# VectorE's order written out around the last depthwise tiles and the first layer norm of a Conformer block

## The chip, the cores and the metric

The kernel runs on one core of one Trainium2 chip. The metric is device time in microseconds of one execution. Three runs of the kernel before gave 2790.43, 2791.1 and 2793.83 us; their median is 2791.1 us.

## The reference

One inference step of a two-layer backbone for 1024 sample tokens and 128 prompt tokens, 1024 features, all in float32. Layer 0 mixes tokens with a Conformer convolution, layer 1 with attention; each is followed by a convolutional feed-forward. The change lies in the Conformer convolution:

```
def conformer_conv(h, w_pw1, dw_w, dw_b, ln_g, ln_b, w_pw2):
    a, g = jnp.split(h @ w_pw1, 2, axis=-1)
    u = a * jax.nn.sigmoid(g)
    u = dwconv(u, dw_w, dw_b)                       # 31 taps over the tokens, feature by feature
    u = jax.nn.silu(layernorm(u, ln_g, ln_b))       # mean and variance over the 1024 features
    return u @ w_pw2
```

A token's layer norm needs all 1024 features, so it can begin only when the depthwise convolution of all features has reached that token. After this, the result goes through `x = x + g1 * y`, a norm, and the feed-forward.

## The kernel before, in words

**Layout.** Features lie on the 128 partitions in 8 tiles (`KT`), tokens along the columns in 3 chunks of 384 (`CH`, `NCH`); chunk 2 ends with the prompt. Matrix products are made to float32 precision from three products of a high and a low part (`mm3`, lines 247 to 249: hi x hi, hi x lo, lo x hi), so every operand of a product exists as a pair `hh`, `hl`. A product of one weight (128 output features) with one chunk is 24 matmuls.

**Depthwise stage.** For tiles 0 to 6, 12 taps run on ScalarE and GpSimd (`taps_pool`, lines 645 to 651) into `pacc`, and 19 on VectorE (`taps_vector`, lines 658 and 660) into `da`, an accumulator of three PSUM banks (tag `acc`, one buffer). `join` (line 666) adds the two and writes `U[c][:, j, :]` for each chunk. For tile 7, the last, 16 taps are matmuls with diagonal matrices (line 706) into one PSUM bank per chunk, `dl[c]` (tag `mm`, four banks, which pw2's products and the layer norm use too), 8 taps run on ScalarE and GpSimd, and 7 on VectorE on top of `dl[c]`, chunk by chunk.

**Layer norm.** The sums for the mean are matmuls with a constant matrix (line 722), seven for the first seven tiles of each chunk, written in the program before any layer norm step. Chunk 0 has its own bank for them; chunks 1 and 2 share a tile of the tag `acc`, which is free when tile 6 has been joined. `layer_norm(c)` then adds the last tile's term (line 726), subtracts the mean in two halves (line 731), squares on ScalarE (line 738, tag `tmp`, two buffers, shared with the squares of pw2's statistics), adds the squares on VectorE for one half and on GpSimd for the other (lines 741 and 744), sums them over the partitions with small matmuls (line 325), raises to the power -0.5 on GpSimd (line 334), spreads the result over the partitions (line 342), scales (line 753), applies Silu (line 757), makes the high part (line 760) and the low part (line 762). It is a generator: `tick()` advances every such generator in `bg` by one step, up to its next `yield`. While the taps of tile 7 for chunk c+1 are written, the norm of chunk c is advanced by one step after each tap.

**After it.** `project_residual` makes the pw2 products (named pw2p in the profile) chunk by chunk and adds them to x (line 384). x comes back from DRAM chunk by chunk (`reload`, line 388) into the place of `U[c]`, so it waits until the layer norm of chunk c is done with it.

**What sets the order.** Every engine works through its own list in order. The lists are made at compile time by a planner that plays the program through with estimated costs and puts an instruction in when its inputs are ready. SyncE's list (all loads of weights and of x) is in the order of the program throughout (`manual_schedule`), TensorE's in the attention alone; within such a region the named engines keep the program's order, and the others stay with the planner. VectorE's list is the planner's everywhere. Next weights are loaded three ahead and split into high and low parts one ahead (lines 209, 220, 221).

Of the kernel before, what the change touches and what calls it, by code (L numbers as in the profile page):

```python
# [16 lines left out]
P = 128  # L17
# [5 lines left out]
CH = 384  # L23
# [40 lines left out]
def raw32(t):  # L64
    return t.bitcast(F32)


def pieces(c):
    """A chunk's columns by the conditioning of their tokens."""
    lo, hi = c * CH, (c + 1) * CH  # L70
    out = []
    if lo < NS:
        out.append((0, min(hi, NS) - lo, 0))
    if hi > NS:
        out.append((max(lo, NS) - lo, CH, 1))
    return out
# [3 lines left out]
def tile_hybrid_step(ctx: ExitStack, tc: tile.TileContext, a: dict, outs: list):  # L80
# [17 lines left out]
    def phase(**slots):  # L98
        """SBUF of a phase: so many tiles of so many columns for each tag."""
        stack = ExitStack()  # L100
        pools = {
            tag: (stack.enter_context(tc.tile_pool(name=f"s_{tag}", bufs=bufs, reuse_waits="tile")), n)
            for tag, (bufs, n) in slots.items()
        }

        def tile_(tag, name, dt=F32, n=None):
            pool_, cols_ = pools[tag]
            return pool_.tile([P, n or cols_], dt, tag=tag, name=name)

        return stack, tile_  # L110
# [15 lines left out]
    class Banks:  # L126
        """PSUM, cut anew for some phases."""

# [16 lines left out]

    # work that runs beside the products, a step after each of them
    bg = []
# [22 lines left out]

    # ---- weights, in the order of their use: loads run up to three tiles ahead, the split into hi + lo (both exact
    # in float32r) one or two ----
    def ffn_order(l):
# [25 lines left out]
    class Weights:  # L199
# [24 lines left out]
        def ahead(self, splits, loads):  # L224
            """Has everything up to so many tiles from the next one split or loaded."""
            for i in range(self.at, min(self.at + max(splits, loads), len(self.order))):
                if self.order[i][0] == "stop":
                    break
                if i < self.at + loads and i not in self.raw and i not in self.ready:
                    self.load(i)  # L230
                if i < self.at + splits and i not in self.ready:
                    self.split(i)
# [17 lines left out]

# [1 line left out]
    def ada(pool, l, grp):  # L252
# [55 lines left out]

# [1 line left out]
    def add_stat(acc, j, c, src, eng=None, tag=None):  # L310
# [8 lines left out]
    def token_rstd(pool, parts, name, bank=None):  # L319
        """Sums over features of all parts[f, token], then (mean + eps) ** -0.5, tokens on partitions."""  # L320
        n = CH // P
        ps = pool("ms", f"{name}_s") if bank is None else bank[:, CH:]
        for t in range(n):
            for i, x in enumerate(parts):
                nc.tensor.matmul(
                    ps[:, t : t + 1], x[:, t * P : (t + 1) * P], ones, start=(i == 0), stop=(i == len(parts) - 1)
                )
        return rstd_of(ps[:, 0:n], 1.0 / D, n, name)
# [8 lines left out]
    def spread(pool, v, name, bank=None):  # L337
        """v[token, t] to every partition, tokens along the columns."""
        n = v.shape[1]
        ps = pool("ms", f"{name}_b") if bank is None else bank  # L340
        for t in range(n):
            nc.tensor.matmul(
                ps[:, t * P : (t + 1) * P], v[:, t : t + 1].to_broadcast([P, P]), ident, start=True, stop=True
            )
        return ps[:, 0 : n * P]
# [44 lines left out]

# [1 line left out]
    def ffn(pool, H, X, l, name, beside, done):  # L392
# [87 lines left out]

    # =========================== layer 0 ===========================
    pool.open(mm=(4, 512), acc=(1, 1536), ms=(1, 512))

# [1 line left out]
    vec_rows = [  # L485
# [36 lines left out]
    def load_x(c):  # L522
        """A chunk's tokens, on partitions, where the low parts of the normed chunks go later."""
        n = CH // P
        toks = hp.tile([P, n, D], F32, tag="hl", name=f"xt{c}")
        for t in range(n):
            tt = c * n + t
            nc.sync.dma_start(
                toks[:, t, :], a["x_sample"][0, tt * P : (tt + 1) * P, :] if tt < NS // P else a["x_prompt"][0]
            )  # L530
        return toks
# [45 lines left out]

    # conformer: gated pointwise, depthwise over tokens, layernorm, silu, pointwise
    us = []

    def gated(j, c):
        """The products of a chunk; yields before their gating."""
        if c == 0:
# [58 lines left out]
    def taps_pool(j, u, pacc, t0, s0_, s1_):  # L642
        """The taps from t0 on, with the bias."""
        d = pacc[:, s0_:s1_]
# [8 lines left out]
    def taps_vector(j, u, d, n, s0_, s1_, fresh):  # L653
        """The first n taps."""
        for t in range(n):
            src = u[:, s0_ + t : s1_ + t]
            if t == 0 and fresh:
                nc.vector.tensor_scalar(d, src, tap(j, t), None, ALU.mult)
            else:
                nc.vector.scalar_tensor_tensor(d, src, tap(j, t), d, ALU.mult, ALU.add)  # L660
            yield
# [9 lines left out]
    for j in range(last + 1):  # L671
# [14 lines left out]
        taps_pool(j, u, pacc, t0, 0, CONV_N)  # L686
        for _ in taps_vector(j, u, da[:, 0:CONV_N], t0, 0, CONV_N, True):
            pass
        for c in range(NCH):
            join(j, da, pacc, c)  # L690

    # the last tile: some taps as products with diagonals, the others on top of them, chunk by chunk, so that the norm
    # of a chunk runs beside the taps of the next
    u = us[last][2]
# [6 lines left out]
    for c in range(NCH):  # L701
        s0_, s1_ = SPAN[c]
        dl.append(pool("mm", f"dl{c}")[:, 0 : s1_ - s0_])
        for i in range(PE_TAPS):
            t = te + i
            nc.tensor.matmul(
                dl[c], diag[:, i, :], u[:, s0_ + t : s1_ + t], start=(i == 0), stop=(i == PE_TAPS - 1)
            )

    L = [None] * NCH  # L710
# [13 lines left out]
    def layer_norm(c):  # L724
# [4 lines left out]
        for g in range(2):  # L729
# [3 lines left out]
            )  # L733
            eng = (nc.vector, nc.gpsimd)[g]
            for i in range(half // 2):
                sq = slot("tmp", f"lnsq{c}_{g}_{i}")[:, 0 : 2 * CH]
# [8 lines left out]
            yield  # L745
        yield
        bank = pool("mm", f"lnv{c}")
        rs = token_rstd(pool, ss, f"lnv{c}", bank)
        yield
        pb = spread(pool, rs, f"lnv{c}", bank)  # L750
        for g in range(2):
            jj = slice(g * half, (g + 1) * half)
            nc.vector.tensor_tensor(
                U[c][:, jj, :], U[c][:, jj, :], pb.unsqueeze(1).to_broadcast([P, half, CH]), ALU.mult
            )
            for j in range(g * half, (g + 1) * half):
                nc.scalar.activation(
                    U[c][:, j, :], U[c][:, j, :], AF.Silu, scale=col("conv_ln_g", j), bias=col("conv_ln_b", j)
                )
            nc.scalar.activation(hh[:, jj, :], U[c][:, jj, :], AF.Copy)  # L760
            yield
            nc.vector.tensor_tensor(hl[:, jj, :], U[c][:, jj, :], raw32(hh)[:, jj, :], ALU.subtract)
# [5 lines left out]
    for c in range(NCH):  # L768
# [4 lines left out]
        if c == 0:  # L773
            tick()

    def project_residual(H, X, c, acc, l, name, tag):
# [29 lines left out]

    # =========================== layer 1 ===========================
    # rotary tables with the norm gains folded in, tokens on partitions; gains: plain, halves swapped and signed
    NB = NS // P + 1
# [59 lines left out]
    def head_norm(ps, which, tt, name):  # L869
        """RMS norm of two heads, rotary unless they are the prompt's; yields between its stages."""  # L870
        ss = tiny(f"{name}ss", 2)
# [37 lines left out]
    def place(b, tt, o):  # L909
        """Heads to [feature, token]."""  # L910
        pt = pool("t", f"ptqk{b}_{tt}")
# [14 lines left out]

    # each slot: the products of a tile, then a further stage of each tile before it, the oldest first
    stages = []
# [50 lines left out]

    # the prompt's queries see the prompt's own keys: the four heads of a group at once  # L980
    def prompt():
# [54 lines left out]

    # samples: blocks of one head and the queries of one chunk, in steps of 128 queries; the scores run two steps
    # ahead of the transposes, the product with V one block behind them
    blocks = [(c, h) for c in range(NCH) for h in range(NH)]
# [27 lines left out]
    def softmax(s, st):  # L1067
        """Yields before each part of its exponential."""
        v = st["v"]
# [121 lines left out]

    # final norm, back to tokens on partitions
    gfs = []
# [44 lines left out]
def _rope_table():  # L1238
    """cos and sin by position on the 64-wide grid: [128, 2, 9, 32]; block t < 8 is the row part of token tile t,
    block 8 the column part, which all tiles share."""  # L1240
    import numpy as np
# [34 lines left out]
```

## Time and profile before

| | us |
|---|---|
| median of three runs | 2791.1 |
| lowest and highest | 2790.43, 2793.83 |
| span of the profiled execution | 2789.3 |
| TensorE busy in the span | 2724.6 (98%) |
| VectorE, ScalarE, GpSimd busy | 1585.4, 1053.5, 699.6 |

The span runs from the first instruction to the last of one profiled execution; a time outside the profile is that of the whole program. Times in the trace are counted from the start of the span. In a timeline row the first number is the start, the second how long the instruction or the merged run of `xN` instructions took, then engine, line, operation and tiles (output<-inputs); brackets give the idle time of the engine before it and who ended it. PE is TensorE (float32 matmuls with plain float32 operands appear as two records each), DVE is VectorE, ACT ScalarE, POOL GpSimd, SPq the queue of SyncE. A busy TensorE need not be at its full clock: the granted clock stands beside it, 1.00 for 2.4 GHz and 0.50 for 1.2 GHz.

### The profile page before, as it was taken

The numbers are of one execution on the slowest core, as the hardware profiler recorded it, in microseconds if no ns is written. First come the engines' busy times: TensorE is split into PE (matmuls) and PEld (weight loads), VectorE is DVE, ScalarE is ACT, GpSimd is POOL, SyncE is SP. The second block draws the span as 40 slices with busy tenths as digits, with TensorE's granted clock in tenths as the row PEclk, the third lists the DMA queues.
The fourth block names the chain that finished last, engine by engine and source line by source line (L and its number), as shares of the span: only waits on it lengthen the run. The fifth ranks groups of instructions, "written<-read, shape, count | busy, mean of one in ns | idle before, by whom it ended". The sixth has DMA issues, their size and how long they took to land.

```text
span 2789.3 us, 40007 instructions
## 1 busy us (share of the span) xinstructions
PE 2724.6 (98%) x15959; PEld 2577.1 (92%) x15959; DVE 1585.4 (57%) x2743; ACT 1053.5 (38%) x2066; POOL 699.6 (25%) x782
## 2 busy tenths in 40 slices
PE   7999989999999999999999899999999999999999
PEld 4867649999999999999999799899999999999998
DVE  6878886544444444445643788766544444444445
ACT  5545546422222221222555777755422122221222
POOL 2777744300000000000555566535000000000003
PEclk9999989999999999999999999999999999999999
DMA  7465425311111111111210000044111111111111
GB/s 261 158 185 160 154 91 176 110 32 46 46 46 46 39 46 38 46 38 46 95 58 1 1 1 1 32 129 136 45 40 46 38 46 39 46 39 45 32 53 69
DMA packets 194419, 192.18 MB, mean 69 GB/s; under 512 B 7072, under 2 KB 173323, under 8 KB 192698
## 3 DMA queue, kind: packets, MB, share of 16 engines
q1 hardware_dynamic: 193946, 189.53, 21.7%
q8 instruction: 126, 2.06, 0.3%
q14 instruction: 59, 0.48, 0.1%
q0 software_dynamic: 288, 0.11, 0.0%
HBM read 175.19 MB, written 14.42 MB: 68 GB/s over the span
## 4 chain that ended last, share of the span: by engine, by line
PE 94%; DVE 3%; DMA 1%; ACT 1%; issue 0%; POOL 0%; SPq 0%; DVEq 0%; ACTq 0%; POOLq 0%
PE f1pd L249 3%; PE f1pd L247 3%; PE f1pd L248 3%; PE f1pg L249 3%; PE f0pg L249 3%; PE f1pg L248 3%; PE f0pg L248 3%; PE f0pv L247 3%; PE f0pg L247 3%; PE f1pv L249 3%; PE f1pg L247 3%; PE f0pv L248 3%; PE f1pv L248 3%; PE f1pv L247 3%; PE f0pv L249 3%; PE f0pd L248 3%
## 5 line engine op out<-in xcount | busy, mean ns | idle before, releaser
L220 ACT ACTIVATE w_hi<-w_raw 128x1024 fp32r<-128x1024 f32 x208 | 218.1, 1058 | 939.4 <-PE f0pd L248 223.7
L221 DVE TENSOR_TENSOR w_lo<-w_raw,w_hi 128x1024 fp32r<-128x1024 f32 x208 | 269.4, 1304 | 425.0 <-ACT w_hi L220 422.4
L651 POOL TENSOR_TENSOR pacc<-pacc,tmp 128x1167 f32<-128x1167 f32 (+2 forms) x98 | 234.2, 2393 | 64.8 <-ACT tmp L650 41.6
L384 DVE SCALAR_TENSOR_TENSOR x<-f1pd,mods,x 128x256 f32<-128x256 f32 (+1 forms) x352 | 170.2, 514 | 102.6 <-PE f1pd L249 102.4
L384 DVE SCALAR_TENSOR_TENSOR x<-f0pd,mods,x 128x256 f32<-128x256 f32 (+1 forms) x352 | 169.8, 514 | 99.1 <-PE f0pd L249 98.9
L660 DVE SCALAR_TENSOR_TENSOR da<-u,dww,da 128x1167 f32<-128x1167 f32 x126 | 180.8, 1435 | 2.8
L1084 POOL TENSOR_TENSOR pr<-pr,sm 128x384 f32<-128x384 f32 x192 | 153.8, 829 | 107.3 <-DVE sm L1082 49.4
L411 POOL MEMSET f1gp<- 128x1 f32 x66 | 3.7, 98 | 703.7 <-DVE f1gp L435 690.5
L411 POOL MEMSET f0gp<- 128x1 f32 x66 | 3.6, 98 | 703.8 <-DVE f0gp L435 690.7
L248 PE MATMUL f1pd<-f1al,w_hi 128*128 128x384 f32 x528 | 178.8, 339 | 0.0
L249 PE MATMUL f1pd<-f1ah,w_lo 128*128 128x384 f32 x528 | 178.7, 338 | 0.0
L249 PE MATMUL f0pd<-f0ah,w_lo 128*128 128x384 f32 x528 | 178.7, 338 | 0.0
L248 PE MATMUL f0pd<-f0al,w_hi 128*128 128x384 f32 x528 | 178.5, 338 | 0.0
L247 PE MATMUL f1pd<-f1ah,w_hi 128*128 128x384 f32 x528 | 178.5, 339 | 0.0
L247 PE MATMUL f0pd<-f0ah,w_hi 128*128 128x384 f32 x528 | 178.0, 338 | 0.0
L249 PE MATMUL f0pg<-n_h,w_lo 128*128 128x384 f32 x528 | 176.7, 335 | 0.0
L249 PE MATMUL f1pg<-n_h,w_lo 128*128 128x384 f32 x528 | 176.7, 335 | 0.0
L248 PE MATMUL f1pg<-n_l,w_hi 128*128 128x384 f32 x528 | 176.7, 335 | 0.0
L248 PE MATMUL f0pv<-n_l,w_hi 128*128 128x384 f32 x528 | 176.7, 335 | 0.0
L248 PE MATMUL f0pg<-n_l,w_hi 128*128 128x384 f32 x528 | 176.7, 335 | 0.0
L247 PE MATMUL f0pg<-n_h,w_hi 128*128 128x384 f32 x528 | 176.7, 335 | 0.0
L247 PE MATMUL f1pg<-n_h,w_hi 128*128 128x384 f32 x528 | 176.7, 335 | 0.0
(327 smaller groups left out, 7802.7 us busy)
## 6 DMA issues: line engine op xcount, KB each, us to landing
adaw<-in_ada_w_dram SPq DMA_DIRECT2D x96, 512.0 KB, 4.4
w_raw<-in_ffn_w_up_dram SPq DMA_DIRECT2D x88, 512.0 KB, 3.8
w_raw<-in_ffn_w_down_dram SPq DMA_DIRECT2D x44, 512.0 KB, 3.9
w_raw<-in_conv_w_pw_dram SPq DMA_DIRECT2D x40, 512.0 KB, 6.8
w_raw<-in_attn_w_o_dram SPq DMA_DIRECT2D x24, 512.0 KB, 4.4
xs_d<-x SPq DMA_DIRECT2D x6, 1536.0 KB, 11.1
x<-xs_d SPq DMA_DIRECT2D x6, 1536.0 KB, 7.8
w_raw<-in_attn_w_qkv_dram SPq DMA_DIRECT2D x12, 512.0 KB, 3.6
```

The lines of the kernel that those rows point to most:

```text
L220: nc.scalar.activation(hi, raw, AF.Copy)
L221: nc.vector.tensor_tensor(lo, raw, raw32(hi), ALU.subtract)
L247: nc.tensor.matmul(ps, wh, mh, start=first, stop=False)
L248: nc.tensor.matmul(ps, wh, ml, start=False, stop=False)
L249: nc.tensor.matmul(ps, wl, mh, start=False, stop=last)
L384: nc.vector.scalar_tensor_tensor(xx, ps[:, lo:hi], mod(l, v, j, cond), xx, ALU.mult, ALU.add)
L411: nc.gpsimd.memset(gp[:, z : z + 1], 0.0)
L651: nc.gpsimd.tensor_tensor(d, d, tmp, ALU.add)
L660: nc.vector.scalar_tensor_tensor(d, src, tap(j, t), d, ALU.mult, ALU.add)
L1084: nc.gpsimd.tensor_tensor(pr[n], pr[n], ri.to_broadcast([P, CH]), ALU.mult)
```

## The change

Three edits; comments and docstrings are taken out besides.

1. From the taps of tile 6 on, up to the end of tile 7's joins, VectorE's list is the order of the program. The VectorE part of tile 6 (19 taps and the joins) is moved in the program behind the products of tile 7 and the diagonal matmuls, to the head of this region. So VectorE makes tile 6 to its end, then the taps of tile 7 for chunk 0 and their join, then the first step of chunk 0's layer norm (line 726, the subtractions), and then the taps of chunk 1, after each of them a step of chunk 0's layer norm, then chunk 2's taps with the steps of chunk 1's.
2. The squares alternate between the two halves, and the subtractions get a step of their own.
3. For chunk 0, scaling, Silu, high and low part go in four parts of two tiles in place of two of four, each low part written after the next part's scaling.

```diff
-        for _ in taps_vector(j, u, da[:, 0:CONV_N], t0, 0, CONV_N, True):
-            pass
-        for c in range(NCH):
-            join(j, da, pacc, c)
+        def on_vector(j=j, u=u, da=da, pacc=pacc, t0=t0):
+            for _ in taps_vector(j, u, da[:, 0:CONV_N], t0, 0, CONV_N, True):
+                pass
+            for c in range(NCH):
+                join(j, da, pacc, c)
+
+        if j < last - 1:
+            on_vector()
...
+    vector = ExitStack()
+    vector.enter_context(tc.manual_schedule(engines={mybir.EngineType.DVE}))
+    on_vector()
+
     L = [None] * NCH
...
-            eng = (nc.vector, nc.gpsimd)[g]
-            for i in range(half // 2):
+        yield
+        for i in range(half // 2):
+            for g in range(2):
+                eng = (nc.vector, nc.gpsimd)[g]
...
             yield
-        yield
         bank = pool("mm", f"lnv{c}")
         rs = token_rstd(pool, ss, f"lnv{c}", bank)
         yield
         pb = spread(pool, rs, f"lnv{c}", bank)
-        for g in range(2):
-            jj = slice(g * half, (g + 1) * half)
+        n = 2 if c == 0 else half
+        for j0 in range(0, KT, n):
+            jj = slice(j0, j0 + n)
             nc.vector.tensor_tensor(
-                U[c][:, jj, :], U[c][:, jj, :], pb.unsqueeze(1).to_broadcast([P, half, CH]), ALU.mult
+                U[c][:, jj, :], U[c][:, jj, :], pb.unsqueeze(1).to_broadcast([P, n, CH]), ALU.mult
             )
...
             nc.scalar.activation(hh[:, jj, :], U[c][:, jj, :], AF.Copy)
-            yield
+            if c or j0 % half:
+                yield
+            if c == 0 and j0:
+                pp = slice(j0 - n, j0)
+                nc.vector.tensor_tensor(hl[:, pp, :], U[c][:, pp, :], raw32(hh)[:, pp, :], ALU.subtract)
+            if c:
+                nc.vector.tensor_tensor(hl[:, jj, :], U[c][:, jj, :], raw32(hh)[:, jj, :], ALU.subtract)
+        if c == 0:
             nc.vector.tensor_tensor(hl[:, jj, :], U[c][:, jj, :], raw32(hh)[:, jj, :], ALU.subtract)
         L[c] = (hh, hl)
...
         if c == 0:
             tick()
+    vector.close()
```

## Rows read from the trace of the kernel before

**Rows 1.** The page's chain of waits, shares of the span by engine.
```profile
PE 94%; DVE 3%; DMA 1%; ACT 1%; issue 0%; POOL 0%; SPq 0%; DVEq 0%; ACTq 0%; POOLq 0%
```

**Rows 2.** Table by stretch: busy us of PE, PEld, DVE, ACT, POOL; clock, DMA.
```profile
402.00:417.00 15.00, 6.18 (x23) 4.92 (x22) 13.06 (x13) 12.81 (x17) 4.02 (x4) 0.50 0.01 2
417.00:422.40 5.40, 5.38 (x17) 5.38 (x18) 2.20 (x2) 5.40 (x8) 0.00 (x0) 0.50 0.51 171
...
422.40:523.70 101.30, 101.30 (x600) 101.30 (x599) 70.93 (x86) 55.98 (x83) 44.22 (x34) 1.00 0.56 169
```

**Rows 3.** Timeline of TensorE, 384 to 417 us.
```profile
384.67 0.81 PE L726 MATMUL mu<-u,mean_w 128*128 128x384 f32 x2
385.32 5.32 PE L722 MATMUL mu<-u,mean_w 128*128 128x384 f32 x16
...
395.53 0.81 PE L726 MATMUL mu<-u,mean_w 128*128 128x384 f32 x2
...
405.87 2.29 PE L325 MATMUL lnv<-ones,lnss 128*128 128x1 f32 x10 [0.28 <-POOL lnss L744]
410.19 1.65 PE L342 MATMUL lnv<-ident,lnv_r 128*128 128x128 f32 x6 [2.02 <-POOL lnv_r L334]
...
417.02 0.69 PE L248 MATMUL pw2p<-ln_l,w_hi 128*128 128x384 f32 x1 [1.37 <-DVE ln_l L762]
```

**Rows 4.** Timeline of VectorE, 337 to 457 us.
```profile
337.73 8.81 DVE L660 SCALAR_TENSOR_TENSOR da<-u,dww,da 128x1167 f32<-128x1167 f32 x6
...
378.53 1.54 DVE L666 TENSOR_TENSOR u<-da,pacc 128x384 f32<-128x384 f32 x4
...
381.05 0.56 DVE L666 TENSOR_TENSOR u<-dl,pacc 128x384 f32<-128x384 f32 x1
...
385.52 3.42 DVE L731 TENSOR_TENSOR u<-u,mu 128x1536 f32<-128x1536 f32 x2 [1.34 <-PE mu L726]
...
415.21 3.42 DVE L762 TENSOR_TENSOR ln_l<-u,ln_h 128x1536 fp32r<-128x1536 f32 x2
...
425.70 0.62 DVE L384 SCALAR_TENSOR_TENSOR x<-pw2p,mods,x 128x384 f32<-128x384 f32 x1 [0.43 <-PE pw2p L249]
427.85 1.23 DVE L221 TENSOR_TENSOR w_lo<-w_raw,w_hi 128x1024 fp32r<-128x1024 f32 x1 [1.53 <-ACT w_hi L220]
...
443.66 3.42 DVE L753 TENSOR_TENSOR u<-u,lnv 128x1536 f32<-128x1536 f32 x2
...
456.78 1.75 DVE L762 TENSOR_TENSOR ln_l<-u,ln_h 128x1536 fp32r<-128x1536 f32 x1
```

**Rows 5.** Timeline of ScalarE, around 410 us and around 1534 us.
```profile
406.71 1.28 ACT L757 ACT_TABLE_LOAD   x1
408.00 4.89 ACT L757 ACTIVATE u<-u,vecs 128x384 f32<-128x384 f32 x8
412.80 2.84 ACT L760 ACTIVATE ln_h<-u 128x1536 fp32r<-128x1536 f32 x2
...
1533.49 1.28 ACT L1080 ACT_TABLE_LOAD   x1
1535.32 0.58 ACT L1080 ACTIVATE pr<-sc,sm 128x384 f32<-128x384 f32 x1 [0.54 <-DVE sm L1072]
```

**Rows 6.** Timeline of GpSimd, 393 to 410 us.
```profile
393.39 2.07 POOL L744 TENSOR_TENSOR lnss<-lnss,lnsq 128x384 f32<-128x384 f32 x2 [1.49 <-ACT lnsq L738]
...
408.90 1.24 POOL L334 TENSOR_TENSOR lnv_r<-lnv_m,mhalf 128x3 f32<-128x3 f32 x1 [3.08 <-DVE lnv_m L332]
```

**Rows 7.** Groups of TensorE by line, 418 to 523.7: busy us, mean ns.
```profile
L325 PE MATMUL lnv<-ones,lnss 128*128 128x1 f32 x12 | 1.4, 236 | 0.0
L342 PE MATMUL lnv<-ident,lnv_r 128*128 128x128 f32 x6 | 0.8, 274 | 0.0
```

**Rows 8.** Timeline of SyncE's queue, at 418.7 us.
```profile
418.66 0.33 SPq L388 DMA_DIRECT2D x<-xs_d  x1
```

**Rows 9.** Timeline of VectorE at 308 us.
```profile
308.11 2.57 DVE L221 TENSOR_TENSOR w_lo<-w_raw,w_hi 128x1024 fp32r<-128x1024 f32 x1
```

More of the change, by code (lines that the diff above doesn't have):

```diff
@@ L750, in layer_norm @@
         pb = spread(pool, rs, f"lnv{c}", bank)
-        for g in range(2):
-            jj = slice(g * half, (g + 1) * half)
+        n = 2 if c == 0 else half
+        for j0 in range(0, KT, n):
+            jj = slice(j0, j0 + n)
             nc.vector.tensor_tensor(
-                U[c][:, jj, :], U[c][:, jj, :], pb.unsqueeze(1).to_broadcast([P, half, CH]), ALU.mult
+                U[c][:, jj, :], U[c][:, jj, :], pb.unsqueeze(1).to_broadcast([P, n, CH]), ALU.mult
             )
-            for j in range(g * half, (g + 1) * half):
+            for j in range(j0, j0 + n):
                 nc.scalar.activation(
```

## The prediction

> **What bounds the kernel now.** I read the page's chain of waits first: 94% of the chain that ended last is TensorE, so the end moves by what TensorE gains or loses [rows 1]. Then the table by stretch around the change: from 402.0 to 422.4 us TensorE's granted clock stands at 0.50 (the 1.2 GHz level), it works for only 6.18 us of the first 15, and from 422.4 to 523.7 it is busy without a break at full clock [rows 2]. At 523.7 the pw2 products end and the feed-forward begins. So this change is worth what it does to the start of that solid block (576 matmuls: 24 for each of 8 weights and 3 chunks), and to how solid the block stays.
>
> Next, who is late in front of the block. In TensorE's timeline there is work up to 396: the diagonal products, the sums for the means (line 722), the last term of chunk 0's mean (line 726) at 384.67, then the sums of chunks 1 and 2, and line 726 of chunk 1 at 395.53 [rows 3]. VectorE's timeline shows the joins of tile 6 as late as 378.53, chunk 0's subtraction of its mean from 385.52, and the last low part of chunk 0 ending at 415.21 + 3.42 = 418.63 [rows 4]. The wait that ends last in front of the block is the one for ln_l, at 417.02 [rows 3].
>
> **What the change moves before the layer norm.** On VectorE tile 6 now runs through first: 19 taps at 1.47 (8.81 for six), 27.9 us, so from 336.3 its joins (1.54) end at 365.7; seven narrower taps of the last tile at no more than 1.47 and a join of 0.56 give 376.6 at the latest, two weight splits at 1.23 that may fall into this stretch 379.1 [rows 4]. That is late for nothing: chunk 0's subtraction needs line 726 on TensorE, and TensorE has work up to 394.9. This slack, 16 us at least, hides all of it, and a split that waits for its load or a dearer row of taps too.
>
> The side effect is on TensorE, whose order the planner still chooses. The rows say by what rule: line 726 of chunk 1 had its join by 381.05 + 0.56, but ran at 395.53, after the sums of chunk 2, which stand earlier in the program [rows 3, 4]. So of what is ready, the earlier line goes first. Line 726 of chunk 0 ran at 384.67 only because the sums for chunks 1 and 2 were not to be had yet: their PSUM tile takes the place of tile 6's accumulator, free only after the joins that began at 378.53. In the new order these joins are done by 366, the sums are ready, and they go ahead of chunk 0's line 726. The same work then ends at 395.53 - 0.65 = 394.88 (line 726 took 0.65 out of it, 384.67 to 385.32), line 726 follows, and the subtraction starts 0.85 later (384.67 to 385.52), at 395.7: **10.2 us later than before**.
>
> **What chunk 0's norm gains.** Before, it took 33.1 us from the subtraction to the last low part (385.52 to 418.63), mixed on VectorE with the norms of the other chunks. Now it runs alone, since the written order holds chunk 1 back. Step by step from the start of the subtraction: 3.4 both halves [rows 4]; 4.5 after one tap and the first add (some 0.5 each, estimated by the join of 384 columns at 381.05); 5.3 the third square, which waits for that add, since its tag has two buffers; 7.0 the fourth; 9.1 GpSimd's last two adds, 2.07 [rows 6]. The new order of the squares is worth under 1 us of this: before, GpSimd's adds ended 9.9 us after the subtraction began. Then 12 small products: TensorE will have idled for 9 us, so I take its 0.50 clock, 0.23 each (2.29 for ten), to 11.9; the power by 13.4 (a small VectorE step and GpSimd's 1.24); the spread in 1.65, to 15.05 [rows 3, 6]. A quarter of the scaling takes 0.9 (an estimate: half of 1.71), to 16.0 [rows 4]. ScalarE's table load, 1.28 us in front of the first Silu at 406.71, is now hidden by ScalarE's waiting: at 1533.49 such a load ran ahead of an instruction that waited on for VectorE [rows 5]. Then ScalarE sets the pace: a quarter is two Silu at 0.61 and half of a 1.42 copy, 1.93 us, four of them 7.7, to 23.7 [rows 5], and the last low part 0.9. That makes 24.7 us, so the norm ends at 420.4, 1.8 us later than before in spite of its quarters.
>
> **What the block gains and loses.** The quarters let TensorE begin earlier within the norm: the first low quarter is there 18.9 us after the subtraction began, at 414.6. From there 18 matmuls, three quarters of the first weight, fit up to 420.4 at the half-clock pace of 0.32 (17 in 5.40 us) [rows 2]. The clock came back 5.4 us after the steady start at 417.02 [rows 2, 3], here then at about 420. So 18 are done at 420.4, against 20 at 422.4 (17, and three of the 23 records before 417): 2.0 us earlier less two at 0.174 (96.7 of the last 101.3 us for 556, an estimate that leaves 4.6 us to small products as in [rows 7]), **1.7 us won**.
>
> Against it stands work that moves into the block. Before, the means' last terms of chunks 1 and 2 and the small products of chunk 1 ran between 395.5 and 411.8, where TensorE waited anyway. Now VectorE's order keeps chunk 1's subtraction behind chunk 0's last low part, so they run inside the block: two line 726 at 0.65 [rows 3], 12 small sums in 1.4 and one spread in 0.8 [rows 7], **3.5 us lost**. Last, SyncE's queue: the reload of x waits until chunk 0's u is free (418.66, 0.03 after the last low part), and the weight loads stand behind it in program order [rows 8]; the first weight that they bring had its low part done at 429.08 [rows 4]. Shifted by 1.8 that is 430.9, while this weight, the fourth, is due at 420.4 + 54 x 0.174 + 0.65 = 430.4 and its low part a little later: **0.3 us lost** (0 to 0.5). Sum: -1.7 + 3.5 + 0.3 = **+2.1 us**.
>
> The profiled span of 2789.3 us becomes 2791.4. The median of the runs shown, 2791.1, lies 1.8 us over that span, for what surrounds it; so I forecast 2793.
>
> **What is late next.** Chunk 1's norm had 25 us to spare and now has little. After 420.4 come a tap, the join and line 726, and its subtraction starts at 422.5. Its halves are strictly in turn, the low part of one before the scaling of the next: 12.9 us to the scaling at full clock (the sum above with the small products at 1.4 and 0.8), then twice 7.3 (1.71, four Silu, 1.42, 1.71), 27.5 in all; the bound above is the 33.1 of chunk 0, which shared its engines. So its last low part ends between 450.0 and 455.6. TensorE wants it at 420.4 + 174 x 0.174 + 2.8 + 12 x 0.174 = 455.6. I take no stall, with 0 to 5.6 us to spare. Chunk 2's norm comes after that; beside products it needs 14.9 us from its scaling to its last low part (443.66 to 456.78 + 1.75) [rows 4], which leaves some 4 us.
>
> **The rivals.**
> *Chunk 0's mean keeps its place on TensorE (chance 0.14).* For it: chunk 0's last join comes early on VectorE now. Against: the rule by program order that the rows show. Then nothing is 10.2 us late: 2.1 - 10.2 = -8.1, 2783.
> *Chunk 1's norm stalls the block, slower (0.20).* The residual of the first weight (line 384, at 425.70 before) needs the reloaded x. If the planner puts it on VectorE ahead of chunk 1's subtraction, that waits for the load, up to 420.5 + 7.0 = 427.5 by the rows, and 0.6 for the residual [rows 4, 8]: the norm ends 5.6 us later, at 455.6 to 461.2, and TensorE stalls 0 to 5.6. At the full price 2.1 + 5.6, 2799; it counts as slower from a stall of 3.5. For it: two of the four PSUM banks of this tag now stay with chunk 2's taps and chunk 1's sums. Against: the residual can as well be placed behind.
> *TensorE stays at full clock through chunk 0's norm (0.08).* The small products then take 1.4 and 0.8 instead of 2.7 and 1.65, 2.1 us less: 2791. Against: it ran at 0.50 from 402 on with work for 6.18 of 15 us [rows 2], and will have less.
> *GpSimd and VectorE block each other in chunk 1's norm (0.05).* A weight split took 2.57 us at 308.11 [rows 9] and 1.23 at 427.85 [rows 4]. As a mechanism of this kernel: three GpSimd adds, each behind a 1.23 us split, put the norm's end 3.7 us later, at 459.3 at the latest, a stall of up to 3.7: 2797. The Trainium skill (SBUF — State Buffer, "SBUF: two separate sides") says that GpSimd and a VectorE instruction with two SBUF inputs take turns on one port pair, each holding it for a whole instruction. By that rule, such blocking is to be expected; the trace agrees at 308.11 and shows most splits free of it.
>
> **How the numbers follow.** My forecast has 0.53, the rivals 0.14, 0.20, 0.08 and 0.05. About 0.2%, 5.6 us, is what a measurement of this kernel can tell from no change. Faster takes the first rival and a sum that is too high: 0.15. Slower takes most of the second rival and the ends of the forecast and the fourth: 0.20. No change has 0.65. The range from 2784 to 2800 holds the forecast and all rivals but the first; the forecast's own range is 2789 to 2797.
>
> **What would show it.** Right: in the trace after, line 726 of chunk 0 stands behind all 42 passes of line 722, near 395; the first subtraction of a mean starts near 396; the last low part of chunk 0 ends some 25 us later; pw2 ends near 525.8. Wrong: line 726 near 385 (first rival), a TensorE wait for ln_h or ln_l after 450 (second or fourth), a granted clock of 1.00 between 402 and 414 (third). A subtraction near 396 with pw2 ending before 520 would break the sum itself.

## The result, and the profile after

The changed kernel takes 2827.3 us (median of three runs, 2825.19 to 2827.97) against 2791.1: a ratio of 1.0132, interval 1.0118 to 1.0147, so it is slower by some 36 us. The forecast was 2793, in a range from 2784 to 2800. Its profiled execution has a span of 2823.4 us.

The chain of waits, by engine, answers to [rows 1]: TensorE's share falls from 94% to 92%, to the gain of engines that it waits for.
```profile
PE 92%; DVE 4%; ACT 2%; DMA 1%; issue 1%; POOL 1%; SPq 0%; DVEq 0%; POOLq 0%; ACTq 0%
```

The table by stretch answers to [rows 2], with the columns given there; the pw2 block is divided at its waits.
```profile
402.00:417.00 15.00, 4.53 (x18) 4.06 (x18) 7.15 (x12) 6.67 (x10) 2.95 (x3) 0.50 0.00 0
417.00:422.40 5.40, 0.00 (x0) 0.00 (x0) 4.18 (x6) 3.28 (x5) 0.00 (x0) 0.50 0.05 9
422.40:431.30 8.90, 2.04 (x4) 0.93 (x5) 7.31 (x10) 3.37 (x4) 1.64 (x2) 0.50 1.04 325
431.30:452.00 20.70, 20.70 (x113) 20.40 (x113) 9.99 (x12) 7.93 (x11) 3.23 (x4) 0.90 0.24 70
452.00:473.20 21.20, 5.42 (x15) 4.25 (x15) 11.29 (x13) 9.23 (x12) 4.88 (x5) 0.60 0.14 42
473.20:559.40 86.20, 86.20 (x512) 86.20 (x512) 59.11 (x76) 47.54 (x73) 37.73 (x28) 1.00 0.48 149
```
TensorE does nothing between 417.0 and 422.4, where before it was in the pw2 block, and from 452.0 to 473.2 it works 5.42 of 21.20 us, in the midst of the block. The last product of pw2 ends at 559.4 (523.9 before): these 35.5 us are the whole loss (36.2 by the medians).

TensorE's timeline (compare [rows 3]) shows where it stands still:
```profile
395.37 0.81 PE L736 MATMUL mu<-u,mean_w 128*128 128x384 f32 x2
...
422.59 1.65 PE L736 MATMUL mu<-u,mean_w 128*128 128x384 f32 x2 [12.64 <-DVE u L666]
430.91 0.56 PE L325 MATMUL lnv<-ones,lnss 128*128 128x1 f32 x2 [6.67 <-DVE lnss L756]
431.33 0.67 PE L247 MATMUL pw2p<-ln_h,w_hi 128*128 128x384 f32 x1
...
460.22 1.65 PE L736 MATMUL mu<-u,mean_w 128*128 128x384 f32 x2 [8.20 <-DVE u L666]
469.45 0.59 PE L325 MATMUL lnv<-ones,lnss 128*128 128x1 f32 x2 [7.58 <-DVE lnss L756]
```
Line 736 is line 726 of before (732 is 722, 741 is 731, 756 is 744, 766 is 753, 770 is 757, 773 is 760, 778 to 782 are 762). The first pw2 product runs at 431.33. It waits for nothing of its own: in front of it in TensorE's list stand line 736 of chunk 1, which waits 12.64 us for chunk 1's last join, and the first small sum of chunk 1's variance, which waits 6.67 us for its squares; 0.42 us after that sum begins the product follows. (The Trainium skill, PSUM — Partial Sum Buffer, "Engine vs sequencer instructions", says that matmuls start in the order of the list; the trace agrees with these 0.42 us after 19.3 us of waiting for others.) The same pair, for chunk 2, stops the block again at 452 and 462.

VectorE's timeline (compare [rows 4]) shows when the inputs were there:
```profile
372.07 1.55 DVE L666 TENSOR_TENSOR u<-da,pacc 128x384 f32<-128x384 f32 x4
...
378.21 0.56 DVE L666 TENSOR_TENSOR u<-dl,pacc 128x384 f32<-128x384 f32 x1
396.21 3.42 DVE L741 TENSOR_TENSOR u<-u,mu 128x1536 f32<-128x1536 f32 x2 [17.45 <-PE mu L736]
...
414.24 0.96 DVE L778 TENSOR_TENSOR ln_l<-u,ln_h 128x768 fp32r<-128x768 f32 x1 [1.90 <-ACT ln_h L773]
...
420.38 0.96 DVE L782 TENSOR_TENSOR ln_l<-u,ln_h 128x768 fp32r<-128x768 f32 x1 [1.11 <-ACT ln_h L773]
...
421.98 0.56 DVE L666 TENSOR_TENSOR u<-dl,pacc 128x384 f32<-128x384 f32 x1
...
424.27 3.42 DVE L741 TENSOR_TENSOR u<-u,mu 128x1536 f32<-128x1536 f32 x2 [1.19 <-PE mu L736]
...
459.55 0.61 DVE L666 TENSOR_TENSOR u<-dl,pacc 128x256 f32<-128x256 f32 x2
```
The first quarter's high part is ready at 414.24 and its low part at 415.2. So the inputs of the first product are there 17 us before it runs.

**Why it stands there.** The list that the compiler made for TensorE has the same order as the trace. This is the changed kernel's around the first and the fifth product of chunk 0, with shortened tile names (3104 and 3300 are the norms of chunks 1 and 2, 3147 and 3317 the first and the fifth product):
```
L736 MATMUL mu<-u_822,mean_w
L325 MATMUL lnv_3104<-ones,lnss_0_3088
L247 MATMUL pw2p_0_3147<-ln_h,w_hi
...
L736 MATMUL mu<-u_823,mean_w
L325 MATMUL lnv_3300<-ones,lnss_0_3216
L247 MATMUL pw2p_4_3317<-ln_h,w_hi
```
Exactly one small sum of each norm goes ahead of a pw2 product, and the other five come after it. That is the sign of a PSUM bank: the small sums of each norm, the pw2 products and `dl` all take their banks from the tag `mm`, whose banks are given out in the program's order. In the program, chunk 1's norm asks for its bank while the taps of chunk 2 are written, before the first pw2 product; chunk 2's norm asks for its own before the fifth. Read so, a product can have its bank only when the earlier asker has begun to use one; runs 1, 2, 9 and 12 test this reading. Before, the order on TensorE was the same: in front of the fifth product, behind 96 pw2 matmuls, stood one small sum of chunk 2. But chunk 2's mean was subtracted by 404.5, the sum did not wait, and the order cost nothing, as VectorE's and TensorE's timelines of before show:
```profile
401.07 3.41 DVE L731 TENSOR_TENSOR u<-u,mu 128x1536 f32<-128x1536 f32 x2
```
```profile
435.72 0.28 PE L325 MATMUL lnv<-ones,lnss 128*128 128x1 f32 x2
```
The written order holds the joins of chunks 1 and 2 back until 422 and 460, and the banks' order passes this on to TensorE. That was the theory with which the experiments began; the rival was that the norms of chunks 1 and 2 are simply late and TensorE would have waited for their results in any case.

### The profile page after: what moved, and what is told of

The parts are those of the page before. It is cut to its first block, busy times and chain, and to the rows that moved or that the text cites. A ratio compares the mean times of both kernels' runs of the same rounds, so it can differ in the third digit from the quotient of the medians.

```text
span 2823.4 us, 40016 instructions
## 1 busy us (share of the span) xinstructions
PE 2725.5 (97%) x15959; PEld 2575.8 (91%) x15959; DVE 1584.9 (56%) x2747; ACT 1054.0 (37%) x2068; POOL 697.8 (25%) x782
## 4 chain that ended last, share of the span: by engine, by line
PE 92%; DVE 4%; ACT 2%; DMA 1%; issue 1%; POOL 1%; SPq 0%; DVEq 0%; POOLq 0%; ACTq 0%
PE f1pd L249 3%; PE f1pd L247 3%; PE f1pd L248 3%; PE f0pg L249 3%; PE f1pg L249 3%; PE f1pg L247 3%; PE f1pv L247 3%; PE f0pg L248 3%; PE f0pv L249 3%; PE f1pg L248 3%; PE f0pv L248 3%; PE f1pv L249 3%; PE f0pg L247 3%; PE f0pv L247 3%; PE f1pv L248 3%; PE f0pd L248 3%
## 5 line engine op out<-in xcount | busy, mean ns | idle before, releaser
L248 PE MATMUL f1pv<-n_l,w_hi 128*128 128x384 f32 x528 | 176.5, 334 | 0.0
```

What stands on the lines that cost most here:

```text
L248: nc.tensor.matmul(ps, wh, ml, start=False, stop=False)
```

## The experiments

All were timed beside runs of the kernel before on the same chip (2788.8 to 2789.7 us there). Line numbers above 700 differ from run to run; the tile names say which step a row is.

**1. Another bank for the norms' small sums.** In the changed kernel:
```diff
-        bank = pool("mm", f"lnv{c}")
+        bank = pool("ms", f"lnv{c}")
```
Expected: 

> The changed kernel, with the layer norm's small PSUM bank (lnv) taken from the tag ms in place of mm. Theory A: banks of the tag mm are handed out in program order; the banks of the norms of chunks 1 and 2 stand in the program ahead of pw2's first and fifth product, so with those norms held back by VectorE's written order TensorE may not start these products. Then this kernel starts pw2 by about 416 us, shows no gap over 3 us at line 736 after 410, ends pw2 at 526 +- 3 and takes 2793 +- 4 us (ratio 1.001). Rival B: the planner put line 736 of chunks 1 and 2 early because its estimate of VectorE is too short, whatever the banks: TensorE waits as before, 2827 +- 4 (1.013). Rival C: the data of chunks 1 and 2 are simply late: pw2 starts early but stalls by as much at the change of chunk, over 2815.

Measured: 2809.11 us, ratio 1.0069 (1.0054 to 1.0084), over theory A's range and under that of rival C. TensorE's waits from 400 to 560 us (total, times, longest):
```profile
PE pw2p L247 <- ACT w_hi L220: 7.6, 5, 3.8
PE lnv L325 <- DVE lnss L756: 6.4, 1, 6.4
PE pw2p L247 <- ACT ln_h L773: 4.3, 1, 4.3
PE pw2p L248 <- DVE ln_l L780: 2.1, 1, 2.1
```
In the changed kernel the two waits for `u` of line 666 come to 20.8 us and those for `lnss` of line 756 to 20.5; here the first are gone, and only chunk 0's own 6.4 us are left of the second. pw2 begins 18.1 us after chunk 0's subtraction (35.1 before this edit), as the prediction had it (18.9 for its low quarter), and in TensorE's timeline it now waits for its own input, with no sum of chunk 1 in front of it:
```profile
415.93 1.01 PE L247 MATMUL pw2p<-ln_h,w_hi 128*128 128x384 f32 x2 [4.31 <-ACT ln_h L773]
```
So the bank is the cause of the stalls, but it is only half of the loss: pw2 still ends at 541.9, behind new waits, mostly for weights.

**2. The same for chunk 2's norm alone.**
```diff
+        bank = pool("ms" if c == 2 else "mm", f"lnv{c}")
```
Expected: 

> The changed kernel, with the small bank of the norm of chunk 2 alone taken from the tag ms. Theory A: the wait in front of pw2's first product stays (first product at 431), the one in front of the fifth (TensorE at 452 to 473, some 19.5 us) goes: 2827 - 19 = 2808 +- 5 (1.006). Rival B (planner's estimate of VectorE): 2827 +- 4 (1.013).

Measured: 2809.84 us, 1.0074 (1.0059 to 1.0089). The stall at 452 to 473 is gone, that in front of the first product stays:
```profile
PE lnv L325 <- DVE lnss L756: 13.0, 2, 6.7
PE mu L736 <- DVE u L666: 12.6, 1, 12.6
```
Each bank thus makes its own stall. The time equals that of run 1 all the same: there pw2 begins 16.6 us earlier than here (415.93 and 432.48) and ends only 1 us earlier (541.89 and 542.86). Run 1 gives back in the block nearly all that it gains at the start, since chunks 1 and 2 are then late for it.

**3. The written order alone**, with the norm's halves and squares as before. In the kernel before:
```diff
+        if j < last - 1:
+            on_vector()
...
+    vector = ExitStack()
+    vector.enter_context(tc.manual_schedule(engines={mybir.EngineType.DVE}))
+    on_vector()
...
+    vector.close()
```

Expected: 

> The kernel before with the first edit alone: VectorE's written order with tile 6 first; the layer norm in halves, as before. Theory A: both waits are there, since they come from the order and the banks: 2825 to 2835 (1.012 to 1.016), the part over the changed kernel being what the quarters save. Rival D: the quarters and the changed steps of the norm make the loss: 2791 to 2797.

Measured: 2832.0 us, 1.015 (1.0133 to 1.0167). The same stall, longer, on TensorE:
```profile
430.83 1.65 PE L735 MATMUL mu<-u,mean_w 128*128 128x384 f32 x2 [16.39 <-DVE u L666]
```
The first edit by itself, the written order with tile 6 first, makes the loss. From the subtraction to the last low part chunk 0's norm takes 31.3 us here (398.31 to 429.59) and 25.1 in the changed kernel: the parts and the squares by turns save 6.2 us of it, of which the ratios, with intervals that overlap, show some 5.

**4. The control: the kernel before with the norms' bank from ms.**
```diff
-        bank = pool("mm", f"lnv{c}")
+        bank = pool("ms", f"lnv{c}")
```

Expected: 

> Control: the kernel before with the layer norm's small bank taken from the tag ms. Theory A: there the norms' banks were handed out long before pw2 asked for its own, so nothing to gain: 2791 +- 4 (1.000). If this bank had been in the way there too, it would be faster by over 0.2%.

Measured: 2790.04 us, 1.0004 (0.9994 to 1.0013). The bank by itself gives nothing that can be told here. The control is not quite clean, since the tag `ms` has one bank only, and this makes a wait of its own in TensorE's waits from 400 to 560:
```profile
PE lnv L325 <- DVE u L753: 3.6, 1, 3.6
```
pw2 begins 31.8 us after chunk 0's subtraction (28.8 before), and from its first product to its last it takes 108.6 us (109.6 before). A gain of some us could hide behind the late start; but in the block of before no small sum is waited for, so there is no stall that the bank could take away.

**5. The four parts and the alternating squares without the written order.**
```diff
-        if j < last - 1:
-            on_vector()
+        on_vector()
...
-    vector = ExitStack()
-    vector.enter_context(tc.manual_schedule(engines={mybir.EngineType.DVE}))
-    on_vector()
...
-    vector.close()
```
Expected: 

> The changed kernel without its written order and with tile 6's VectorE work at its old place: what stays are the norm's end in four parts for chunk 0 and the squares taken by turns. Theory A (the loss comes from the order alone, and the quarters release the first product of pw2 some 4 to 8 us earlier, which the first product can use only as far as VectorE's stages of chunks 1 and 2 let it): 2784 to 2792 us, no slower than before (2791). Rival B (the four parts cost by themselves, by more small instructions on VectorE among the chunks' norms): 2793 to 2800 us.

Measured: 2797.1 us, 1.0028 (1.0016 to 1.004). Slower, against theory A. pw2 begins 2.1 us earlier (412.2), but in the block TensorE's timeline has
```profile
441.37 0.58 PE L325 MATMUL lnv<-ones,lnss 128*128 128x1 f32 x2 [9.25 <-DVE lnss L752]
```
which is the first sum of chunk 2's norm, again ahead of the fifth product. The expected rival, more small instructions on VectorE, has the time in its range but does not explain a wait at this place; runs 9 and 12 test the bank for it.

**6. Run 1 with chunk 0's mean first**: the sums of chunks 1 and 2 are written behind chunk 0's first norm step.
```diff
-    for c in range(NCH):
...
+    def sums(c, mu):
...
+    sums(0, pool("mm", "mu0"))
...
+            mu_all = pool("acc", "mu").rearrange("p (c n) -> p c n", c=NCH)
+            for cc in range(1, NCH):
+                sums(cc, mu_all[:, cc])
```
Expected: 

> The changed kernel with the small bank of the norms taken from the tag ms, as in the run before, and besides with the mean sums of chunks 1 and 2 written behind chunk 0's first norm step, so that line 736 of chunk 0 no longer stands behind them on TensorE. Theory A (the prediction's step: the sums ahead of the mean hold chunk 0's subtraction by 10 us, and these 10 us go straight into the start of pw2): 2798 to 2802 us, 8 to 11 us below the run with the bank alone (2809). Rival C (the queue of weights behind the reloads, and chunks 1 and 2, set the end, and an earlier chunk 0 only lengthens TensorE's later waits): 2805 to 2810 us.

Measured: 2801.61 us, 1.0044 (1.0029 to 1.0059), 7.5 us under run 1. The step "10.2 us later" was thus a real cost. The mean comes only part of the way forward: of the 28 records of line 732 (here 727) for chunks 1 and 2, 20 run behind it, and VectorE's wait in front of the subtraction falls from 17.63 us in run 1 to 9.77 here, by 7.9 us and not 10.2. By the medians about as much reaches the end.

**7. Run 6 with a short written order**, closed behind chunk 0's subtraction.
```diff
         if c == 0:
             tick()
+            vector.close()
...
-    vector.close()
```
Expected: 

> As the run with the bank from ms and the mean first, and with the written order of VectorE closed right behind chunk 0's subtraction: tile 6, chunk 0's taps, its join and its subtraction are in the written order, chunks 1 and 2 and the norms are left to the planner again. Theory A (the written order of chunks 1 and 2 is what stretches their norms, from the forecast 27 to 33 us to 38 us, and what puts the reload and the weights behind it late): 2784 to 2793 us. Rival (the later chunks lose by tile 6 being first or by the shared queue, not by their written order): 2797 to 2803 us.

Measured: 2792.62 us, 1.0011 (1.0002 to 1.0021), 9.0 us under run 6. VectorE's timeline has the subtractions of chunks 0 and 1 together and chunk 2's soon after, and chunk 1's last low part at 439.26 where run 1 has it at 463.25:
```profile
394.34 6.75 DVE L738 TENSOR_TENSOR u<-u,mu 128x1536 f32<-128x1536 f32 x4 [8.41 <-PE mu L733]
402.89 3.41 DVE L738 TENSOR_TENSOR u<-u,mu 128x1536 f32<-128x1536 f32 x2
...
439.26 1.75 DVE L777 TENSOR_TENSOR ln_l<-u,ln_h 128x1536 fp32r<-128x1536 f32 x1
```
(Line 738 is the subtraction here, 777 the low part.) So the theory is right on the place and only half right on the mechanism: chunk 1's norm is no shorter (43 us from 397.7), it begins 30 us earlier, before chunk 0's scaling. What makes it slow in run 1, once begun, is seen in that run's VectorE timeline:
```profile
448.16 1.75 DVE L766 TENSOR_TENSOR u<-u,lnv 128x1536 f32<-128x1536 f32 x1 [0.61 <-PE lnv L342]
...
450.37 0.61 DVE L384 SCALAR_TENSOR_TENSOR x<-pw2p,mods,x 128x384 f32<-128x384 f32 x1
451.02 1.23 DVE L221 TENSOR_TENSOR w_lo<-w_raw,w_hi 128x1024 fp32r<-128x1024 f32 x1
454.25 0.62 DVE L384 SCALAR_TENSOR_TENSOR x<-pw2p,mods,x 128x384 f32<-128x384 f32 x1 [2.01 <-PE pw2p L249]
454.93 1.76 DVE L780 TENSOR_TENSOR ln_l<-u,ln_h 128x1536 fp32r<-128x1536 f32 x1
456.61 1.75 DVE L766 TENSOR_TENSOR u<-u,lnv 128x1536 f32<-128x1536 f32 x1
```
The low part of chunk 1's first half stands behind a residual (line 384) which itself waits 2.01 us for TensorE's product, and the second half's scaling stands behind that low part. The norm takes 37.7 us in this way (427.30 to 465.01). This was read from the trace; the late beginning and the slow course were not told apart. Nor does run 7 keep what run 6 gained: only 4 of the 28 records of the sums run behind chunk 0's mean, and the subtraction starts at 394.34 (391.43 in run 6). Its 9.0 us are won in spite of that.

**8. Run 1 with a weight loaded ahead of each reload.**
```diff
+        weights.ahead(0, RING + 1)
         X[c] = reload(0, c, "x1_")
```
Expected: 

> The changed kernel with the norms' small bank from ms, and with one more weight tile loaded ahead of each chunk's reload on SyncE's queue. Theory A (what is left of the loss after the bank, 18 us, is in good part the weights that stand on SyncE behind a reload that waits for the chunk's last low part: TensorE's waits for w_hi of 1.0, 1.2, 3.8 and 1.1 us and the half clock that follows them): the w_hi waits of 431 to 433 and 471 to 477 go or halve, 2799 to 2804 us. Rival (chunk 1's and 2's late low parts set the end; a weight that is there earlier only waits for them): 2807 to 2811 us.

Measured: 2806.0 us, 1.0063 (1.0046 to 1.008), between the two ranges; 3 us under run 1 by the medians, with intervals that overlap. The theory named the right queue and the wrong cause:
```profile
PE pw2p L247 <- ACT ln_h L773: 6.1, 2, 4.3
PE pw2p L248 <- DVE ln_l L780: 4.0, 2, 3.0
PE n_b L342 <- POOL n_r L334: 2.5, 1, 2.5
PE pw2p L247 <- ACT w_hi L220: 1.5, 2, 1.0
```
The waits for `w_hi` fall from 7.6 to 1.5 us, and waits for the norms' parts take their place (4.3 of the first row is the start of pw2, as in run 1). The weights were merely what came last; behind them stand the late norms of chunks 1 and 2.

**9. Run 5 with the bank from ms**.
```diff
-        bank = pool("mm", f"lnv{c}")
+        bank = pool("ms", f"lnv{c}")
```
Expected: 

> The four parts alone, as run before (2797, 8 us over the kernel before, its pw2 block started 2.1 us earlier, at 412.2, but TensorE waited 9.25 us at 432.1 for the squares of chunk 2's norm and ran 10.2 us at half clock after it), and the small bank of the norms from the tag ms. Theory A (that wait is the bank again: pw2's fifth product could get its bank only behind the bank of chunk 2's norm): the 9.25 us wait goes, and with it the half clock, 2783 to 2787 us, faster than before by 1 to 2 tenths of a per cent. Rival (chunk 2's norm itself is late with the four parts, and TensorE waits for its low parts instead): 2790 to 2797 us.

Measured: 2788.2 us, 0.9993 (0.9984 to 1.0001), 8.9 us under run 5 and 1.2 us over theory A's range. The stall in the block is gone, so it was the bank; but pw2 begins at 416.57, 29.0 us after chunk 0's subtraction (26.7 in run 5), behind a new wait at the start:
```profile
414.01 2.69 PE L325 MATMUL lnv<-ones,lnss 128*128 128x1 f32 x12 [3.73 <-DVE u L762]
```
This is chunk 1's norm; the tag `ms` has one bank, which is free only when chunk 0's scaling (line 762 there) has read it.

**10. Run 9 with the weight ahead**, by the line of run 8.

Expected: 

> As the run with the four parts and the bank from ms, with one more weight tile loaded ahead of each reload. Theory A (a weight behind a reload costs time only where the reload is issued late in its chunk, as with the written order): within 2 us of the run without it. Rival (the waits for weights at each chunk's start of some 1 us each are on the path): 2 to 4 us less.

Measured: 2787.49 us, 0.9991 (0.9982 to 1.0), 0.7 us from run 9: no difference that can be told.

**11. Run 7 with the weight ahead**, by the same line.

Expected: 

> As the run with the bank from ms, the mean first and the written order closed behind chunk 0's subtraction (2792.6), with one more weight tile loaded ahead of each reload. Theory A (with chunks 1 and 2 back with the planner one wait of 1.56 us for a weight's low part is left in the block): 2790 to 2793 us. Rival (the weights' place decides more): under 2788 us.

Measured: 2790.74 us, 1.0002 (0.9994 to 1.0011); 1.9 us under run 7 by the medians, with intervals that overlap.

**12. Run 5 with the bank from ms for chunk 2's norm alone.**
```diff
-        bank = pool("mm", f"lnv{c}")
+        bank = pool("ms" if c == 2 else "mm", f"lnv{c}")
```
Expected: 

> As the run with the four parts and the bank from ms, but only chunk 2's norm takes its bank from there, chunks 0 and 1 keep the tag mm. With ms for all three, the wait of 9.25 us at 432 was gone, but pw2 began at 416.6 instead of 412.2, behind a wait of 3.73 us of chunk 1's small sums (line 325) for chunk 0's scaling, since the tag ms has one buffer. Theory A (both waits are banks handed out in the program's order): pw2 begins near 412 and TensorE has no wait of more than 2 us in the block; 2782 to 2786 us. Rival (the start at 416.6 has another cause, the planner's order of VectorE): 2786 to 2790 us, as with ms for all.

Measured: 2784.13 us, 0.9981 (0.9972 to 0.999): faster than the kernel before by some 5 us (3 to 8), and than the changed one. TensorE's timeline and its table by stretch:
```profile
406.01 2.72 PE L325 MATMUL lnv<-ones,lnss 128*128 128x1 f32 x12 [5.76 <-DVE lnss L752]
...
408.60 1.31 PE L247 MATMUL pw2p<-ln_h,w_hi 128*128 128x384 f32 x3
```
```profile
402.00:417.00 15.00, 10.99 (x54) 10.99 (x54) 9.69 (x13) 7.95 (x13) 1.75 (x2) 0.67 0.28 100
417.00:422.40 5.40, 5.40 (x33) 5.40 (x33) 2.65 (x3) 5.40 (x9) 0.00 (x0) 1.00 1.14 298
422.40:516.40 94.00, 93.88 (x554) 93.27 (x553) 74.01 (x87) 58.40 (x87) 47.93 (x34) 1.00 0.53 160
```
pw2 begins 25.7 us after chunk 0's subtraction (382.87) and not 28.8 as before (414.32 - 385.52), the block has no wait of note, and it ends at 516.4. Counted from the subtraction that is 133.5 us against 138.4: 4.8 us, about the gain that the times show (5.2). The remaining 2.7 us of the earlier end were there before the subtraction began, in front of the part that was changed. The four parts and the squares by turns were not run apart, nor the kernel before with chunk 2's bank alone; that the gain is theirs and not the bank's is argued from the block of before, which has no stall for the bank to take away.

## Why the prediction was wrong

**Right.** Tile 6 first is covered: its joins end at 373.6 (forecast 365.7; a weight split that waited 5.5 us for its high part and another of 2.02 us stood in the way) and tile 7's join of chunk 0 at 378.8, while VectorE then waits 17.45 us for TensorE. The planner's rule holds: line 736 of chunk 0 runs behind all the sums, at 395.37, and the subtraction starts at 396.2 (forecast 395.7). Chunk 0's norm takes 25.1 us (24.7) and ends at 421.3 (420.4). That this agrees so closely is in part luck: the first Silu comes 14.8 us after the subtraction began, 1.2 us sooner than the sum had it, and ScalarE's four quarters then take 9.4 us, 1.7 us more, since a copy of two tiles takes 0.84 us and not half of 1.42 and ScalarE waits 1.16 us for VectorE on the way. The table load is hidden, as ScalarE's timeline shows (compare [rows 5]):
```profile
402.54 1.28 ACT L770 ACT_TABLE_LOAD   x1
410.97 2.50 ACT L770 ACTIVATE u<-u,vecs 128x384 f32<-128x384 f32 x4 [7.15 <-DVE u L766]
```

**Wrong.** The step that has the first low quarter there at 414.6 and lets 18 matmuls fit from there up to 420.4 took it that pw2 begins when its inputs are there. They were there, at 415.2. But it begins 17.0 us later than before (431.33 after 414.32), because its bank comes after the bank of chunk 1's norm. The step "I take no stall" fails for the same reason at the fifth product: 8.20 + 7.58 = 15.8 us of the 18.5 by which the block from its first product to its last is longer; the other 2.7 us are the half clock and the small products that moved in, not taken apart. These two steps hold the whole loss of 35.5 us. The prediction had the parts in hand: it said that the written order keeps chunk 1's subtraction behind chunk 0's last low part, and that two of four banks stay with chunk 2's taps and chunk 1's sums; it did not ask in which order the program hands out the others.

Behind that error lies a second, which the bank hid. With the bank taken away (run 1), the time from the subtraction to the end of pw2 is 144.0 us (397.87 to 541.89), not the 130.1 forecast; 9.7 of these 13.9 us are TensorE's waits in the block. The term that was too small is chunk 1's norm: 27.5 to 33.1 us were given, 37.7 measured, and in its VectorE timeline stand the residuals and weight splits that the program mixes among its steps, some of them waiting for TensorE. It ends at 465.01; the reload for chunk 1 is issued at 465.04, the weights stand behind it, and the longest wait for one of them, 3.8 us, ends at 475.52. The 0.3 us for a weight behind the reload stood for up to 7.6 us of waits, but run 8 shows that they cover the late norms.

By the ratios, at 27.9 us for each per cent, the loss of 36.8 us comes apart roughly so (the interval of each ratio is some 3 to 4 us to either side): 17.6 the banks (1.0132 to 1.0069, run 1), 7.0 the mean behind the sums (to 1.0044, run 6), 9.2 the written order beyond chunk 0, less what run 7 gives back of run 6's gain (to 1.0011), 3.1 left. In what is left a wait of 3.7 us for the one bank of ms stands in run 7's trace, as in run 9; in run 7 it was not tried by itself. The parts are one path through the edits; in another order they would be of other sizes, as run 2 shows, where chunk 2's bank alone gives as much as all three.

**The rivals.** That chunk 0's mean keeps its place did not come, but as an experiment it was worth 7.5 us where 10.2 was said, with the mean brought forward in part. The slower rival had the right side and chunk, but another mechanism: no residual waited for the reload ahead of chunk 1's subtraction, and TensorE waits for no `ln_h` or `ln_l` after 450. The full clock did not come (0.50 from 402). For GpSimd and VectorE blocking each other, the group of VectorE's weight splits from 402 to 560 (durations least, median, longest, in ns) has:
```profile
L221 DVE TENSOR_TENSOR w_lo<-w_raw,w_hi x23: 1206/1226/1835, 439.8 to 556.2; 128x1024 fp32r<-128x1024 f32 x23
```
Eighteen of the 23 take 1.21 to 1.23 us. The five that begin while a GpSimd instruction is running (at 495.04, 515.05, 518.30, 545.29 and 548.99) take 1.38 to 1.83; where the split is first, it keeps its time. The four inside chunk 1's norm (439.80 to 454.78) meet no GpSimd instruction, so this rival did not come either. In run 1 a part of it did: inside chunk 1's norm one split took 1.49 us and another 2.04, both begun beside a running GpSimd add, and GpSimd's first add took 2.09 us beside a third split (1.00 in chunk 0's norm). In the changed kernel a split at 368.60 took 2.02 us while GpSimd's adds ran from 368.49 to 372.60, in front of the norms and under cover. (The Trainium skill, SBUF — State Buffer, "SBUF: two separate sides", says that of two such instructions the one that starts first has the port pair for all its length and the other is blocked; the trace agrees in these five splits and in the one at 368.60.)

## What to carry to other kernels

Before an order is written out for one engine, list what the other engines' instructions in that stretch take from shared pools, in the order of the program: a product whose inputs are ready can still wait for an earlier asker of its tag to begin. If one small instruction of a late stage stands alone in front of a block, look for a bank, and give that stage a bank of another tag (here 18 us, and with the four parts alone the step from a loss to a gain). Count the banks of the other tag too: with one for all three norms, 3.7 us came back as a wait. And keep a written order as short as what it is for: what the program mixes into the region (residuals, splits) is ordered too, and waits there for its own producers.

## What the runs showed of the hardware

In the changed kernel the stall inside the block cost more than its length. The table by stretch, divided finer:
```profile
435.70:452.00 16.30, 16.30 (x100) 16.00 (x98) 9.98 (x11) 7.93 (x11) 1.88 (x2) 1.00 0.25 75
452.00:456.00 4.00, 0.02 (x1) 0.00 (x0) 4.00 (x5) 3.11 (x5) 0.00 (x0) 1.00 0.30 88
456.20:473.10 16.90, 5.29 (x14) 4.15 (x15) 7.29 (x8) 5.92 (x8) 4.88 (x5) 0.50 0.11 32
473.30:480.00 6.70, 6.70 (x44) 6.70 (x43) 1.92 (x3) 1.47 (x2) 2.46 (x2) 1.00 0.11 30
```
TensorE stops at 452.0 at full clock; from 456.2 the granted clock is 0.50 (1.2 GHz), and the 5.29 us of work up to 473.1, between and behind the two waits, run at that level: the pw2 matmuls follow each other there every 0.32 us, and every 0.17 us from 473.3 on, where the clock is 1.00 again. In run 12, without a stall in the block, the clock stays at 1.00 from 417 to its end.
